# A plain first gate/up pair and down's stores issued from ScalarE's queue, in a one-core hybrid decoder step

## The chip, the cores and the metric

One core of a Trainium2 chip runs the whole program. The metric is the device time of one execution in microseconds (us). Before the change it is 1429.11 us, the median of three runs (1429.8, 1425.21, 1429.11).

## The reference

One inference step of a one-layer decoder: a mixer (gated MLP over chunks beside a Mamba-2 scan), cross-attention into 256 memory tokens, then the feed-forward network. 1024 prompt tokens and 8 sample tokens go through it (1032 columns), model width 1024, hidden width 2816, all in float32. The change is in the feed-forward network, and at its start in the norm ahead of it:

```python
def rmsnorm(x, g):
    xf = x.astype(f32)
    y = xf * lax.rsqrt(jnp.mean(xf * xf, -1, keepdims=True) + EPS)
    return (y * g.astype(f32)).astype(x.dtype)
def swiglu(hn, w_gate, w_up, w_down):
    return (jax.nn.silu(hn @ w_gate) * (hn @ w_up)) @ w_down
```

## The kernel before

**Numbers.** A float32 product is made of three fp32r matmul passes over a high and a low part of each operand (`mm3`, L170: hi by hi, hi by lo, lo by hi). Splitting an operand is a cast on ACT (the high part, L275 or L146) and a subtraction on DVE or POOL (the low part, L276 or L147).

**Where the change begins.** The last stage before the feed-forward network is cross-attention's output projection, second half (`stage(..., XO, ev_xo, name="xob")`, L1423). Its evacuation `norm_evac` (L906) adds the residual, squares, and after the eighth block asks for the norm's factor by `lagged_rstd` with the pair of lags `LAG_N = (14, 20)`, counted in matmuls that `mm3` issues: a row sum on PE (`m_csn`, L236), square root and reciprocal on ACT and DVE (`rsbn`, `rsan`, `crvn`, L219 to L224), and a spread of the factor over the partitions on PE (`m_crn`, L279). Then `quarters` (L1183) multiplies the columns by it. There are three column chunks (512, 256 and 264 wide), numbered 0, 1, 2 behind `csn3` and `crn3`. `combine(0)` makes the operands of column half q = 0 (chunk 0), `combine(1)` those of q = 1 (chunks 1 and 2).

**Gate and up** run by one level of Strassen: the hidden blocks are taken in 11 pairs, the model width in two halves, the columns in two halves q, each half of two quarters (256 wide, in q = 1 264). Seven products P1 to P7 take the place of eight. `items` (L1208) lists the work: first gate and up of pair 0 for q = 0 alone, then gate and up of pairs 1 to 10 for both q, with pair 0's q = 1 in between after pair 6. `prepare` (L1226) makes one operand of the weights two to five products ahead: sums of the four 128x512 pieces of the raw weight tiles `fr` (`ws`, L1237 to L1240, on DVE for the first four items and on POOL after), and the split into `fw`. `gate_up` (L1255) issues a product as 12 matmuls into a PSUM bank for each q (`g_..` for q = 0 and `m_..` for q = 1, X, Y, Z) and evacuates each: P1 is copied on ACT (`t`, L1283), P6, P7, P5, P4, P3 are added on DVE (L1285, L1292 to L1298), Silu is on ACT. A raw weight tile (`raw`, two buffers) comes by `load_pair` (L1220) on SP's queue.

**What down needs is made beside it.** `down_operands` (L1319) forms differences of a finished pair's hidden values (`dx`, L1324) and stores them and the values to DRAM, two DMAs for each pair and q (`x_d<-u`, `x_d<-dx`, L1331). `load_down` (L1349) loads a pair's two raw blocks of down's weights (`dr`), `down_sums` (L1356) forms sums `ds` of them and stores these (`s_d<-ds`, L1362). `dr`, `ds` and `dx` share one tag `qu` of four buffers, in rotation, so that `ds` of one pair is written where the `dx` was that the store L1331 of the pair before is still reading. All these DMAs are issued from SP's in-order queue, as are the weights' loads.

```python
                nc.sync.dma_start(x_d[i : i + m, fp, :, 256 * q : 256 * q + w].rearrange("o p n -> p o n"), src)
```

A scheduler sets each engine's order of instructions from the order in which they are written and their priorities.

Of the kernel before, what the change touches and what calls it, by code (L numbers as in the profile page):

```python
# [9 lines left out]
F32R = mybir.dt.float32r  # L10
# [7 lines left out]
P = 128  # L18
D = 1024
# [24 lines left out]
def hymba_step(ctx: ExitStack, tc: tile.TileContext, I, O):  # L44
# [55 lines left out]
    def add(w, n, k=KT):  # L100

        first = len(panels)
        panels.extend(w[j].rearrange("p (k n) -> p k n", k=k) for j in range(n))
        return first
# [9 lines left out]
    P_QA = add(I["w_q"], 8)  # L114
    P_QB = add(I["w_q"], 8)
    P_XO = [add(I["w_xo"], 8) for _ in range(2)]
    NPAIR = NF // 2

    raws, split = {}, {}
# [136 lines left out]
    def lagged_rstd(lags, use, pool, accs, ci, scale, nm):  # L256

        v = []

        def sums():  # L260
            sp = col_sums(accs, ci, nm)
            with tc.high_priority():
                v.append(pool.tile([P, len(accs), len(windows(ci))], F32, tag="crv", bufs=2, name=f"crv{nm}"))
                rstd(pool, v[0], sp, scale, nm)
            later(lags[1], rows)

        def rows():
            with tc.high_priority():
                rb = spread(v[0], ci, nm)
            use(rb)  # L270

        later(lags[0], sums)
# [630 lines left out]

    def norm_evac(accs, H, gi, XN, spill, nm, use=None, tmps=None):  # L906

        acc = {}
        pool = nrm

        def evac(j, ci, ps):
            w = CH[ci][1] - CH[ci][0]
            h = H[ci][j // 4][:, j % 4, :]
            with tc.high_priority():
                nc.vector.tensor_add(h, h, ps)
                if j == 0:
                    acc[ci] = accs[ci].tile([P, 512 if accs[ci] is nrm else w], F32, tag=f"acc{'' if accs[ci] is nrm else ci}", bufs=1, name=f"{nm}acc{ci}")
                    nc.scalar.activation(acc[ci][:, :w], h, AF.Square)
                else:
                    sq = pool.tile([P, 512], F32, tag="nsq", bufs=2, name=f"{nm}sq{ci}_{j}")  # L920
                    nc.scalar.activation(sq[:, :w], h, AF.Square)
                    eng = nc.gpsimd if j < 6 and nm == "n1" else nc.vector
                    eng.tensor_tensor(acc[ci][:, :w], acc[ci][:, :w], sq[:, :w], op=ALU.add)
            if spill is not None and j % 4 == 3:
                nc.sync.dma_start(spill[:, j - 3 : j + 1, CH[ci][0] : CH[ci][1]], H[ci][j // 4])
            if j == 7:
                lagged_rstd(LAG_N, lambda rb: (use or normed)(ci, rb[0]), pool, [[acc[ci]]], ci, 1.0 / D, f"{nm}{ci}")

        def normed(ci, rb):
            w = CH[ci][1] - CH[ci][0]  # L930
            hi = [hs(ci, F32R, f"{nm}h{ci}_{i}") for i in range(2)]
            lo = [hs(ci, F32R, f"{nm}l{ci}_{i}") for i in range(2)]
            for k in range(KT):
                i, kk = k // 4, k % 4
                tmp = n2.tile([P, 512], F32, tag=tmps[0], bufs=2, name=f"{nm}t{ci}_{k}")
                nc.vector.scalar_tensor_tensor(tmp[:, :w], H[ci][i][:, kk, :], vecT[:, k, gi : gi + 1], rb[:, :w], op0=ALU.mult, op1=ALU.mult)
                split_from(hi[i][:, kk, :], lo[i][:, kk, :], tmp[:, :w], nc.gpsimd if k % 2 else None)
            XN[ci] = xof((hi, lo))

        return evac  # L940

    quarters = None
    with ExitStack() as c2:
# [185 lines left out]

        H2 = [None] * 3  # L1130
        n3accs = [nrm] * 3
        ev_xo = norm_evac(n3accs, H2, V_FFN, None, h2_d, "n3", lambda ci, rb: quarters(ci, rb))
        XO = [lambda k, ci=ci: (OS[ci][0][k // 4][:, k % 4, :], OS[ci][1][k // 4][:, k % 4, :]) for ci in range(3)]

        def h2(ci):
# [12 lines left out]
    with ExitStack() as c3:  # L1148
# [6 lines left out]
        def piece(nm, tag="gu"):  # L1155
            return n3.tile([P, 4, 264], F32, tag=tag, bufs=4, name=nm)

        def operand(q, nm):

            if nm == ORDER[-1]:  # L1160
                return [n3.tile([P, 4, 264], F32R, tag="op", bufs=4, name=f"s{nm}{x}{q}")[:, :, : WQ[q]] for x in "hl"]
            if q == 0:
                t = hsp.tile([P, 2, 4, 256], F32R, tag="hs0", bufs=6, name=f"s{nm}0")
                return [t[:, i] for i in range(2)]
            return [hsp.tile([P, 4, 264], F32R, tag=f"hs{i}", bufs=6, name=f"s{nm}{i}1") for i in (1, 2)]
# [21 lines left out]
        def combine(q):  # L1187

            b11, b21, b12, b22 = (B[q, half, i] for half in range(2) for i in range(2))

            def part(nm, src, eng=nc.vector):
                XQ[q][nm] = operand(q, nm)
                split_from(*XQ[q][nm], src, eng)

            part("P1", b11)
            nc.vector.tensor_tensor(b11, b12, b11, op=ALU.subtract)
            part("P5", b11)
            nc.vector.tensor_tensor(b11, b22, b11, op=ALU.subtract)
            part("P6", b11)
            part("P2", b21)  # L1200
            nc.vector.tensor_tensor(b12, b22, b12, op=ALU.subtract)
            part("P7", b12)
            nc.vector.tensor_tensor(b21, b21, b11, op=ALU.subtract)
            part("P4", b21)
            part("P3", b22)


        items = [(x, 0, (0,)) for x in "gu"]  # L1208
        for fp in range(1, NPAIR):
            items += [(x, fp, (0, 1)) for x in "gu"] + ([(x, 0, (1,)) for x in "gu"] if fp == 6 else [])  # L1210
        wraw, wsum, wop = {}, {}, {}
# [9 lines left out]

        def order_of(n):

            return ORDER if n > 3 else ("P1", "P2", "P6", "P7", "P5", "P4", "P3")

        def prepare(step):  # L1226

            n, o = divmod(step, 7)
            if n >= len(items):
                return  # L1230
            load_pair(n)
            (a11, a12), (a21, a22) = ((t[:, 0:512], t[:, 512:D]) for t in wraw[n])
            nm = order_of(n)[o]
            if nm == "P6":
                eng = nc.vector if n < 4 else nc.gpsimd
                s1, s2, s3, s4 = wsum[n] = [n3.tile([P, 512], F32, tag="ws", bufs=4, name=f"ws{n}_{i}") for i in range(4)]
                eng.tensor_tensor(s1, a21, a22, op=ALU.add)  # L1237
                eng.tensor_tensor(s2, s1, a11, op=ALU.subtract)  # L1238
                eng.tensor_tensor(s4, a12, s2, op=ALU.subtract)
                eng.tensor_tensor(s3, a11, a21, op=ALU.subtract)  # L1240
            src = {"P1": a11, "P2": a12, "P4": a22}[nm] if nm in ("P1", "P2", "P4") else wsum[n][("P5", "P6", "P7", "P3").index(nm)]
            t = wp.tile([P, D], F32R, tag=("whi", "wlo")[step % 2], name=f"fw{step}")
            split_from(t[:, 0:512], t[:, 512:D], src)
            wop[step] = tuple(t[:, s].rearrange("p (k n) -> p k n", n=P) for s in (slice(0, 512), slice(512, D)))
            if o == 6:
                load_pair(n + 1)
# [69 lines left out]

        differences = []

        def down_operands(fp, q, r):  # L1319

            w = WQ[q]
            r = r.rearrange("p j h n -> p (j h) n")
            t = piece(f"dx{fp}_{q}", "qu")[:, 0:3, :w]
            sub = lambda o, x, y: nc.vector.tensor_tensor(o, x, y, op=ALU.subtract)  # L1324
            sub(t[:, 1], r[:, 3], r[:, 1])
            sub(r[:, 1], r[:, 1], r[:, 0])
            sub(t[:, 0], r[:, 3], r[:, 1])
            sub(t[:, 2], r[:, 2], t[:, 0])
            for i, src in ((0, r), (4, t)):
                m = src.shape[1]  # L1330
                nc.sync.dma_start(x_d[i : i + m, fp, :, 256 * q : 256 * q + w].rearrange("o p n -> p o n"), src)  # L1331

        def form_differences():
            for work in differences:
# [16 lines left out]
        def down_sums(fp):  # L1351

            (a11, a12), (a21, a22) = ((t[:, 0], t[:, 1]) for t in dn[fp])
            t = [n3.tile([P, 2, 512], F32, tag="qu", bufs=4, name=f"ds{fp}_{i}") for i in range(2)]
            s1, s2, s3, s4 = t[0][:, 0], t[0][:, 1], t[1][:, 0], t[1][:, 1]
            op = lambda o, x, y, k: nc.vector.tensor_tensor(o, x, y, op=k)  # L1356
            op(s1, a21, a22, ALU.add)
            op(s2, s1, a11, ALU.subtract)
            op(s3, a11, a21, ALU.subtract)
            op(s4, a12, s2, ALU.subtract)  # L1360
            for i in range(2):
                nc.sync.dma_start(s_d[2 * i : 2 * i + 2, :, fp, :].rearrange("s p n -> p s n"), t[i])  # L1362

        def prepare_down(n):

# [55 lines left out]
            return t[:, 0, i], t[:, 1, i]  # L1421

        stage(plan_of(P_XO[1], 8, first=(1, 2), last=(1, 2), chunks=(1, 2)), XO, ev_xo, name="xob")  # L1423
        for n in range(len(items)):
            gate_up(n, between_of(n))
        form_differences()
# [212 lines left out]
```

## Time and profile before

| | us |
|---|---|
| median of three runs | 1429.11 |
| the profiled execution's own time | 1433.45 |
| its span (first to last instruction) | 1431.7 |
| PE busy | 1373.5 (96%) |
| DVE busy | 967.6 (68%) |
| ACT busy | 627.3 (44%) |
| POOL busy | 365.5 (26%) |
| mean granted TensorE clock | 0.984 |

Span and time differ by what lies around the first and last instruction. In the profile's rows a start is in us from the span's start; "idle before <-releaser" is the time that an engine stood still before an instruction, and what ended it; L is a line of the program. SPq and ACTq are the queues from which DMAs are issued.

### The profile page before, as it was taken

The numbers are of one execution on the slowest core, as the hardware profiler recorded it, in microseconds if no ns is written. First come the engines' busy times: TensorE is split into PE (matmuls) and PEld (weight loads), VectorE is DVE, ScalarE is ACT, GpSimd is POOL, SyncE is SP. The second block draws the span as 40 slices with busy tenths as digits, with TensorE's granted clock in tenths as the row PEclk, the third lists the DMA queues.
The fourth block names the chain that finished last, engine by engine and source line by source line (L and its number), as shares of the span: only waits on it lengthen the run. The fifth ranks groups of instructions, "written<-read, shape, count | busy, mean of one in ns | idle before, by whom it ended". The sixth has DMA issues, their size and how long they took to land. (4 is left out here: it accounts for less than half of the span.)

```text
span 1431.7 us, 26080 instructions
## 1 busy us (share of the span) xinstructions
PE 1373.5 (96%) x10291; PEld 1308.1 (91%) x10291; DVE 967.6 (68%) x2021; ACT 627.3 (44%) x1141; POOL 365.5 (26%) x289
## 2 busy tenths in 40 slices
PE   8999999999999989999979999999899999999997
PEld 8889988899998968978979999999899999999997
DVE  7875689734524876578988766676765665655685
ACT  5666545234423545744464332232332343544654
POOL 3321122201121524320001434334443431003020
PEclk9999999999999999999999999999999999999998
DMA  8531243311733487377324554434546569655664
GB/s 301 186 96 61 91 126 104 97 45 48 248 133 99 154 288 269 106 269 276 104 89 144 170 159 138 142 118 140 170 159 201 171 189 317 206 184 171 203 194 133
DMA packets 145531, 232.67 MB, mean 163 GB/s; under 512 B 8328, under 2 KB 91880, under 8 KB 145024
## 3 DMA queue, kind: packets, MB, share of 16 engines
q1 hardware_dynamic: 145264, 230.94, 49.8%
q8 instruction: 81, 1.33, 0.4%
q14 instruction: 42, 0.34, 0.1%
q10 hardware_dynamic: 144, 0.05, 0.0%
HBM read 179.16 MB, written 51.81 MB: 161 GB/s over the span
## 5 line engine op out<-in xcount | busy, mean ns | idle before, releaser
L146 ACT CAST wh<-wr 128x1024 fp32r<-128x1024 f32 (+1 forms) x85 | 88.0, 1038 | 85.3 <-PE g_gv L170 25.1
L275 ACT CAST fw<-ws 128x512 fp32r<-128x512 f32 x96 | 59.2, 620 | 137.8 <-POOL ws L1238 61.6
L276 DVE TENSOR_TENSOR fw<-ws,fw 128x512 fp32r<-128x512 f32 x96 | 88.9, 928 | 41.3 <-ACT fw L275 41.0
L147 DVE TENSOR_TENSOR wl<-wr,wh 128x1024 fp32r<-128x1024 f32 x59 | 75.9, 1289 | 28.3 <-ACT wh L146 28.1
L147 POOL TENSOR_TENSOR wl<-wr,wh 128x1024 fp32r<-128x1024 f32 (+1 forms) x26 | 62.8, 2415 | 112.2 <-ACT wh L146 67.3
L275 ACT CAST fw<-fr 128x512 fp32r<-128x512 f32 x72 | 44.5, 618 | 79.5 <-PE m_uZ L170 20.7
L1237 POOL TENSOR_TENSOR ws<-fr 128x512 f32<-128x512 f32 x20 | 26.8, 1341 | 200.4 <-DMA fr<-in_w_gate_dram 120.8
L276 DVE TENSOR_TENSOR fw<-fr,fw 128x512 fp32r<-128x512 f32 x72 | 59.5, 826 | 9.6 <-ACT fw L275 9.1
L1542 PE MATMUL m_d<-xP,dwhi 128*128 128x264 f32 x448 | 64.1, 285 | 0.0
L276 DVE TENSOR_TENSOR dwlo<-dw,dwhi 128x1024 fp32r<-128x1024 f32 x32 | 39.8, 1245 | 35.1 <-ACT dwhi L275 35.0
L1542 PE MATMUL g_d<-xP,dwhi 128*128 128x256 f32 x448 | 63.0, 283 | 0.0
L276 DVE TENSOR_TENSOR xP<-xsP,xP 128x512 fp32r<-128x512 f32 (+2 forms) x84 | 55.0, 696 | 11.4 <-ACT xP L275 9.8
L170 PE MATMUL m_uY<-sP,fw 128*128 128x264 f32 (+1 forms) x432 | 58.4, 284 | 2.1 <-DVE fw L276 1.5
L170 PE MATMUL g_gY<-sP,fw 128*128 128x256 f32 (+1 forms) x432 | 58.4, 283 | 1.7 <-DVE t L1292 1.7
L1542 PEld LDWEIGHTS m_d<-xP,dwhi 128*128 128x128 f32 x448 | 58.5, 189 | 0.0
L1542 PEld LDWEIGHTS g_d<-xP,dwhi 128*128 128x128 f32 x448 | 57.7, 191 | 0.0
L170 PEld LDWEIGHTS m_uY<-sP,fw 128*128 128x128 f32 x432 | 54.6, 189 | 2.7 <-DVE fw L276 1.7
L170 PEld LDWEIGHTS g_gY<-sP,fw 128*128 128x128 f32 x432 | 54.3, 190 | 2.4 <-DVE t L1292 2.3
L1304 POOL TENSOR_TENSOR u<-u,g 128x512 f32<-128x512 f32 (+1 forms) x22 | 30.1, 1372 | 100.4 <-DVE u L1296 99.5
L275 ACT CAST dwhi<-dw 128x1024 fp32r<-128x1024 f32 x32 | 33.6, 1051 | 48.7 <-PE m_d L1542 38.5
L275 ACT CAST xP<-xsP 128x512 fp32r<-128x512 f32 (+2 forms) x84 | 45.2, 588 | 21.4 <-DMA xsP<-x_d 12.2
L170 PE MATMUL m_gY<-sP,fw 128*128 128x264 f32 x360 | 49.2, 285 | 4.9 <-DVE t L1292 4.9
(520 smaller groups left out, 3918.5 us busy)
## 6 DMA issues: line engine op xcount, KB each, us to landing
xsP<-x_d SPq DMA_DIRECT2D x35, 520.0 KB, 5.6
wr<-in_w_q_dram SPq DMA_DIRECT2D x24, 512.0 KB, 4.0
fr<-in_w_gate_dram SPq DMA_DIRECT2D x24, 512.0 KB, 3.6
fr<-in_w_up_dram SPq DMA_DIRECT2D x24, 512.0 KB, 3.7
dr<-in_w_down_dram SPq DMA_DIRECT2D x22, 512.0 KB, 6.4
s_d<-ds SPq DMA_DIRECT2D x22, 512.0 KB, 3.2
wr<-in_w_in_dram SPq DMA_DIRECT2D x20, 512.0 KB, 4.0
dw<-s_d SPq DMA_DIRECT2D x20, 512.0 KB, 4.5
```

The costliest lines, as they stand in the source:

```text
L146: nc.scalar.copy(hi[:, s], r[:, s])
L147: (nc.gpsimd if i == 0 or P_QA <= i < P_XO[1] else nc.vector).tensor_tensor(lo[:, s], r[:, s], f(hi[:, s]), op=ALU.subtract)
L170: ins = nc.tensor.matmul(ps, lhs(k)[a], rhs(k)[b], start=(fresh and i == 0), stop=(i == n - 1), skip_group_check=not (fresh and done))
L275: nc.scalar.copy(dst_hi, src)
L276: (eng or nc.vector).tensor_tensor(dst_lo, src, f(dst_hi), op=ALU.subtract)
L1237: eng.tensor_tensor(s1, a21, a22, op=ALU.add)
L1304: nc.gpsimd.tensor_tensor(t, t, gates[q][:, 1, :, :], op=ALU.mult)
L1542: nc.tensor.matmul(ps[:, : WQ[q]], wdn[n](k)[a], x_at(nm, q, k)[b], start=(i == 0), stop=(i == 3 * NPAIR - 1))
```

## The change

1. Pair 0, q = 0 is taken out of `items`. A new `first_pair()` runs it ahead of them without Strassen: for gate and up, each of two hidden blocks, each of two column quarters, one group of 24 matmuls (three passes over eight blocks of the model width). Its weights come as whole panels through `split_panel` (L146, L147; L148, L149 after), so no sums and no products P1 to P7 have to be made or added for it. It needs one operand more, the quarter B12, and P2, B12 and P3 ahead of the others.
2. `prepare` makes the weights' sums on DVE for two items where it was four, which are the same two items as before without the first two.
3. The second lag of the norm ahead of it goes from 20 to 44.
4. The stores of L1331 (44 DMAs) and L1362 (22 DMAs) are issued from ACT's queue.

```diff
-                lagged_rstd(LAG_N, lambda rb: (use or normed)(ci, rb[0]), pool, [[acc[ci]]], ci, 1.0 / D, f"{nm}{ci}")
+                lagged_rstd(lag, lambda rb: (use or normed)(ci, rb[0]), pool, [[acc[ci]]], ci, 1.0 / D, f"{nm}{ci}")
-        ev_xo = norm_evac(n3accs, H2, V_FFN, None, h2_d, "n3", lambda ci, rb: quarters(ci, rb))
+        ev_xo = norm_evac(n3accs, H2, V_FFN, None, h2_d, "n3", lambda ci, rb: quarters(ci, rb), lag=(14, 44))
+            if nm == "B12":
+                return [n3.tile([P, 4, 264], F32R, tag="gu", bufs=4, name=f"s{nm}{x}{q}")[:, :, : WQ[q]] for x in "hl"]
-            part("P1", b11)
+            if q == 0:
+                for nm, b in (("P1", b11), ("P2", b21), ("B12", b12), ("P3", b22)):
+                    part(nm, b)
+            else:
+                part("P1", b11)
-        items = [(x, 0, (0,)) for x in "gu"]
+        items = []
-            return ORDER if n > 3 else ("P1", "P2", "P6", "P7", "P5", "P4", "P3")
+            return ORDER if n > 1 else ("P1", "P2", "P6", "P7", "P5", "P4", "P3")
-                eng = nc.vector if n < 4 else nc.gpsimd
+                eng = nc.vector if n < 2 else nc.gpsimd
+        def first_pair():
+            for x, p0 in (("g", P_G0), ("u", P_U0)):
+                r = piece(f"{x}0_0")[:, :, :256].rearrange("p (j h) n -> p j h n", j=2)
+                for j in range(2):
+                    ahead(p0 + j)
+                    if p0 + j == P_U0:
+                        load_pair(0)
+                    if p0 + j == P_U0 + 1:
+                        for s in range(3):
+                            prepare(s)
+                    hi, lo = split[p0 + j]
+                    for half in range(2):
+                        ps = (gbank, mbank)[half](f"{x}0_{j}_{half}")
+                        ops = [XQ[0][nm] for nm in (("P1", "P2"), ("B12", "P3"))[half]]
+                        mm3(ps[:, :256], lambda k: (hi[:, k, :], lo[:, k, :]), lambda k: tuple(t[:, k % 4, :] for t in ops[k // 4]), range(KT))
+                        with tc.high_priority():
+                            if x == "g":
+                                nc.scalar.activation(r[:, j, half, :], ps[:, :256], AF.Silu)
+                            else:
+                                nc.vector.tensor_mul(r[:, j, half, :], gates[0][:, j, half, :], ps[:, :256])
+                gates[0] = r if x == "g" else None
+            differences.append(lambda: down_operands(0, 0, r))
-                nc.sync.dma_start(x_d[i : i + m, fp, :, 256 * q : 256 * q + w].rearrange("o p n -> p o n"), src)
+                nc.scalar.dma_start(x_d[i : i + m, fp, :, 256 * q : 256 * q + w].rearrange("o p n -> p o n"), src)
-                nc.sync.dma_start(s_d[2 * i : 2 * i + 2, :, fp, :].rearrange("s p n -> p s n"), t[i])
+                nc.scalar.dma_start(s_d[2 * i : 2 * i + 2, :, fp, :].rearrange("s p n -> p s n"), t[i])
+        first_pair()
```

The scheduler decides what this does to the orders. Three places follow.

PE at the start of the feed-forward network, before. `g_gZ0_0` and `m_uX0_0` are products of pair 0's gate and up, `m_csn32` and `m_crn32` the row sum and the spread of chunk 2's norm factor, `m_crn31` the spread of chunk 1's.

```order
L170 MATMUL g_gY0_0_7880<-sP40_7307,fw5_7827 128x256 x12
L170 MATMUL g_gZ0_0_7967<-sP3h0_7310,fw6_7844 128x256 x4
L170 MATMUL g_gZ0_0_7967<-sP3l0_7311,fw6_7844 128x256 x4
L170 MATMUL g_gZ0_0_7967<-sP3h0_7310,fw6_7844 128x256 x4
L279 MATMUL m_crn31_0_7762<-ident_72,crvn31_7728 128x128 x2
L236 MATMUL m_csn32_7853<-ones_77,n3acc2_7358 128x1 x3
L279 MATMUL m_crn32_0_7891<-ident_72,crvn32_7857 128x128 x3
L170 MATMUL m_uX0_0_8022<-sP10_7288,fw7_7877 128x256 x12
```

The same place now; `g_u0_1_0` is the plain group of up's hidden block 1, column quarter 0. From the row of `m_csn32` to that of `m_crn32` there are 18 rows of 4 matmuls; the first and the last rows of that stretch are:

```order
L238 MATMUL m_csn32_7830<-ones_77,n3acc2_7362 128x1 x3
L172 MATMUL m_g0_0_1_7854<-sB12h0_7323,wh84_7657 128x256 x4
L172 MATMUL m_g0_0_1_7854<-sP3h0_7327,wh84_7657 128x256 x4
```

```order
L172 MATMUL g_u0_1_0_8062<-sP10_7317,wl87_7986 128x256 x4
L172 MATMUL g_u0_1_0_8062<-sP20_7320,wl87_7986 128x256 x4
L281 MATMUL m_crn32_0_7897<-ident_72,crvn32_7834 128x128 x3
L172 MATMUL m_g0_1_1_7958<-sB12h0_7323,wh85_7794 128x256 x4
```

Chunk 2's row sum and the spread of its factor stood next to each other on PE; now 72 matmuls of 256 columns stand between them.

SP through one pair, before: stores of pair 4 (`u4`, `dx4`; the last digit is q), the loads and sums of down's pair 5, and gate/up's weights `fr11`, `fr12`.

```order
L1220 DMA fr11_0_10151<-in_w_up_dram 128x1024
L1331 DMA x_d_102<-u4_0_9870 128x4x256
L1349 DMA dr5_0_10367<-in_w_down_dram 128x1024
L1220 DMA fr11_1_10152<-in_w_up_dram 128x1024
L1349 DMA dr5_1_10368<-in_w_down_dram 128x1024
L1331 DMA x_d_102<-dx4_0_10252 128x3x256
L1331 DMA x_d_102<-u4_1_9871 128x4x264
L1331 DMA x_d_102<-dx4_1_10259 128x3x264
L1362 DMA s_d_103<-ds5_0_10503 128x2x512
L1220 DMA fr12_0_10402<-in_w_gate_dram 128x1024
L1362 DMA s_d_103<-ds5_1_10504 128x2x512
```

The same pair now, on SP and then on ACT (`fr9` and `fr10` are the same weights, the items being two fewer):

```order
L1231 DMA fr9_0_10123<-in_w_up_dram 128x1024
L1384 DMA dr5_0_10339<-in_w_down_dram 128x1024
L1231 DMA fr9_1_10124<-in_w_up_dram 128x1024
L1384 DMA dr5_1_10340<-in_w_down_dram 128x1024
L1231 DMA fr10_0_10374<-in_w_gate_dram 128x1024
```

```order
L1366 DMA x_d_102<-u4_0_9842 128x4x256
L1294 COPY t00_10081<-g_gX5_0_10092 128x256
L1294 COPY t01_10084<-m_gX5_1_10106 128x264
L277 CAST fw62_10120<-ws8_3_9946 128x512
L1366 DMA x_d_102<-dx4_0_10224 128x3x256
L1366 DMA x_d_102<-u4_1_9843 128x4x264
L1366 DMA x_d_102<-dx4_1_10231 128x3x264
L277 CAST fw63_10155<-fr9_0_10123 128x512
L1299 ACTIVATE g5_0_10087<-g_gX5_0_10092 128x256
```

On SP the load `dr5_0` now follows the load of `fr9_0` directly; on ACT the store of `u4_0` stands ahead of both copies of P1, and three stores ahead of the next cast. SP's list has 423 rows where it had 489, ACT's 1158 where it had 1104.

## Rows read from the trace of the kernel before

**Rows 1.** The profile's page, busy time and share of the span by engine.

```profile
PE 1373.5 (96%) x10291; PEld 1308.1 (91%) x10291; DVE 967.6 (68%) x2021; ACT 627.3 (44%) x1141; POOL 365.5 (26%) x289
```

**Rows 2.** Windows by stage: PE, PEld, DVE, ACT, POOL busy (instructions), PEclk, DMA share, GB/s.

```profile
718.00:787.00 69.00, 58.56 (x474) 57.89 (x474) 60.49 (x115) 35.65 (x58) 6.57 (x6) 0.95 0.35 116
787.00:1140.00 353.00, 339.75 (x2782) 335.31 (x2781) 232.73 (x415) 106.66 (x209) 138.09 (x103) 1.00 0.50 159
1140.00:1196.00 56.00, 56.00 (x469) 56.00 (x468) 37.20 (x66) 20.26 (x37) 18.47 (x14) 1.00 0.66 199
```

**Rows 3.** Timeline of PE, 730 to 744 us, around the norm's last spread.

```profile
730.32 0.73 PE L236 MATMUL m_csn<-ones,n3acc 128*128 128x1 f32 x6
739.09 0.87 PE L279 MATMUL m_crn<-ident,crvn 128*128 128x128 f32 x3 [8.04 <-DVE crvn L224]
739.61 2.67 PE L170 MATMUL m_uX<-sP,fw 128*128 128x256 f32 x12
742.12 1.60 PE L170 MATMUL m_uY<-sP,fw 128*128 128x256 f32 x12
743.56 1.24 PE L170 MATMUL m_uZ<-sP,fw 128*128 128x256 f32 x9
```

**Rows 4.** Timelines of ACT and of DVE, 730 to 740 us.

```profile
736.12 1.05 ACT L275 CAST sP<-B 128x1056 fp32r<-128x1056 f32 x1
```

```profile
731.80 3.22 DVE L1183 SCALAR_TENSOR_TENSOR B<-H,vecT,m_crn 128x256 f32<-128x256 f32 x8
737.20 1.26 DVE L276 TENSOR_TENSOR sP<-B,sP 128x1056 fp32r<-128x1056 f32 x1 [1.42 <-ACT sP L275]
...
739.09 0.69 DVE L1237 TENSOR_TENSOR ws<-fr 128x512 f32<-128x512 f32 x1
```

**Rows 5.** PE's waits, 760 to 1200 us: total, times, longest.

```profile
PE m_gY L170 <- DVE t L1292: 4.9, 6, 1.7
...
PE g_uY L170 <- DVE t L1292: 1.5, 2, 1.0
...
PE g_gZ L170 <- DVE g L1294: 1.1, 6, 0.2
```

**Rows 6.** DVE's waits, 760 to 1200 us.

```profile
DVE ds L1356 <- DMA x_d<-dx: 34.8, 8, 6.5
```

**Rows 7.** Timeline of SP, 872 to 905 us: one pair's DMA issues.

```profile
877.04 0.38 SPq L1331 DMA_DIRECT2D x_d<-u  x1
...
880.46 0.42 SPq L1331 DMA_DIRECT2D x_d<-dx  x1
...
881.46 1.93 SPq L1331 DMA_DIRECT2D x_d<-dx  x1
```

**Rows 8.** Timelines of DVE, PE and ACT in the same pair.

```profile
888.76 0.78 DVE L1356 TENSOR_TENSOR ds<-dr 128x512 f32<-128x512 f32 x1 [6.48 <-DMA x_d<-dx]
892.89 0.42 DVE L1292 TENSOR_TENSOR t<-t,m_gY 128x264 f32<-128x264 f32 x1
```

```profile
880.74 1.59 PE L170 MATMUL g_gX<-sP,fw 128*128 128x256 f32 x12
893.36 1.73 PE L170 MATMUL m_gY<-sP,fw 128*128 128x264 f32 x12 [1.73 <-DVE t L1292]
```

```profile
876.59 0.37 ACT L1283 COPY t<-g_gX 128x256 f32<-128x256 f32 x1 [0.81 <-PE g_gX L170]
```

**Rows 9.** Windows of two us in the same pair (columns as in rows 2).

```profile
879.00:881.00 2.00, 2.00 (x19) 2.00 (x19) 1.93 (x6) 0.06 (x1) 0.00 (x0) 1.00 1.01 270
...
887.00:889.00 2.00, 2.00 (x19) 2.00 (x18) 0.24 (x1) 0.00 (x0) 1.92 (x2) 1.00 1.03 329
```

**Rows 10.** The line L1331, and the one DMA that ACT issues.

```profile
DMA to landing us min/median/max: 2.6/8.1/10.3
```

```profile
0.80 0.40 ACTq L84 DMA_DIRECT2D vecT<-in_vecs_dram  x1
1.23 1.28 ACT L302 ACT_TABLE_LOAD   x1 [1.23 <-PEq L1628]
```

More of the change, by code (lines that the diff above doesn't have):

```diff
@@ L116, in hymba_step @@
     P_XO = [add(I["w_xo"], 8) for _ in range(2)]
+    P_G0 = add(I["w_gate"], 2)
+    P_U0 = add(I["w_up"], 2)
     NPAIR = NF // 2
@@ L901, in hymba_step, with norm_evac @@
         stage([([(P_GU + j, j)], (0, 1, 2)) for j in range(2)] + [([(P_GU + j, j) for j in (2, 3)], (0, 1, 2))], X, ev_um, name="gu")
-    def norm_evac(accs, H, gi, XN, spill, nm, use=None, tmps=None):
+    def norm_evac(accs, H, gi, XN, spill, nm, use=None, tmps=None, lag=LAG_N):
         acc = {}
@@ L1199, in combine @@
             part("P6", b11)
-            part("P2", b21)
+            if q == 1:
+                part("P2", b21)
             nc.vector.tensor_tensor(b12, b22, b12, op=ALU.subtract)
@@ L1204, in combine @@
             part("P4", b21)
-            part("P3", b22)
-        items = [(x, 0, (0,)) for x in "gu"]
+            if q == 1:
+                part("P3", b22)
+        items = []
         for fp in range(1, NPAIR):
```

## The prediction

> **What bounds the kernel now.** First the page's busy times: PE works 96% of the span and every other engine at most 68% [rows 1], so an edit is worth what it takes off PE's work or off PE's idle time. Then the windows by stage show where the idle time lies. In the start of the feed-forward network (718 to 787 us) PE is busy 58.56 of 69.00, so 10.44 us are lost; in gate and up (787 to 1140) 339.75 of 353.00, so 13.25; from 1140 to 1196 it is busy throughout [rows 2]. Those two losses are all that this change can win back. Next the timeline of the first: one gap of 8.04 us, in which PE waits for the last norm factor [rows 3]. The clock granted in this stage is 0.95 of full speed where later it is 1.00 [rows 2]: after the gap the twelve matmuls of `m_uX` hold PE until the next twelve start, 742.12 - 739.61 = 2.51 us, while those next twelve take 743.56 - 742.12 = 1.44 [rows 3], another 1.07 lost. Last PE's waits in the second stretch, and what stands behind them: the longest are waits for the DVE addition `t` of P7 [rows 5], and DVE was late because it stood 34.8 us in eight pairs before `ds`, waiting for the store `x_d<-dx` to let go of a buffer [rows 6].
>
> **One pair, to see that chain.** The store of `u` is issued at 877.04 and six more DMAs follow by 881.46 on the same queue (first, fifth and last are shown [rows 7]). They are 512 KB (`u`, both `dr`, `fr`), 384 (`dx`), 528 and 396 KB: 3356 KB. The DMA engines are busy all this while, at 1.01 to 1.03 in the windows shown [rows 9]. DVE starts `ds` at 888.76 after 6.48 us of waiting, behind it come the additions, the last at 892.89, and PE starts `m_gY` 1.73 us late at 893.36 [rows 8].
>
> **The change, part by part.**
>
> Arithmetic. The first pair for q = 0 takes 2 x 2 x 2 groups of 24 = 192 matmuls where Strassen took 2 x 7 x 12 = 168. A matmul of 256 columns is 1.44 / 12 = 0.120 us [rows 3], so 24 more cost 24 x 0.120 = **+2.9**, all on PE, which nothing hides.
>
> The gap before the norm's spread. Before, nothing of PE's stands between the row sum and the spread; now 72 matmuls do, 72 x 0.120 = 8.6 us, more than the 8.04 of the gap [rows 3]. That the chain itself grows is unlikely: before, it shared ACT with table loads (1.28 each [rows 10]) and a cast (1.05), and DVE with eight multiplications (3.22) and a split (1.26) [rows 4]. DVE loses here 8 sums and 14 splits at 0.69 and 11 evacuations at 0.42, 19.8 us, and gains four panel splits and one of B12 at about 1.26, and four evacuations at 0.42: 8.0 [rows 4, 8]. I take **-8.0** for the gap and, since PE then doesn't stand still before, **-1.1** for the clock.
>
> What is late next. The 10.44 - 8.04 = 2.4 us of other idle time in this stage will not stay as it is. The items that follow now start their sums and casts behind the plain panels, on a raw buffer that comes free only when the last panel is split. Laying the new order on the durations, I find PE early in three places: twice where an operand of q = 1 waits for its cast and split (1.05 + 1.26 [rows 4]), 1.8 and 1.9 us, and once where a cast stands behind the first store in ACT's queue, 0.8. That is an estimate of 4.5 us, so **+2.1** against 2.4; its bounds are none left (-2.4) and as much again as the gap (+8). The three sums of the first stage: 2.9 - 8.0 - 1.1 + 2.1 = **-4.1**, from -8.6 (all 11.5 us gone, 2.9 paid) to +2.9 plus little.
>
> The later lag (20 to 44) only places the spread; it is the 72 matmuls above, and I cost it at nothing beyond them. The operands made earlier are the same work; B12 is one cast and one split more, in the 8.0 above.
>
> The stores leave SP's queue. Three things follow. `dr_0` no longer stands behind the store of `u`, which waits for DVE; what it waits for itself are the transfers of the pair before, so it goes right behind the load that precedes it, and its 512 KB are out of the crowd: 2844 KB are left. The loads of weights don't stand behind the stores of `ds` any more. And `dx_0` has on its own queue only `u_0` ahead of it. The 3356 KB from 877.04 to 888.76 moved at 286 KB/us [rows 7, 8]; if `dx` lands with the last byte of 2844 KB it is there at 877.04 + 9.9 = 887.0, and if it lands with `u_0`, itself and the two loads beside them (512 + 384 + 512 + 512 = 1920 KB) at 883.8. When does it have to land? From the start of `ds` to the end of the last addition are 892.89 + 0.42 - 888.76 = 4.55 us, and PE would have been ready at 893.36 - 1.73 = 891.63 [rows 8], so `ds` must start by 887.1. Even the late end meets that, just; the early one by 3 us. The waits that hang on this are 4.9 + 1.5 + 1.1 = 7.5 [rows 5]; I take 7 of them, and 1 of the 13.25 - 7.5 = 5.7 that remain, where casts wait for weights that came late. That is **-8.0**, from 0 to -13.25.
>
> What the issue costs on ACT. On SP an issue takes about 0.4 us, and 1.93 at the longest in this pair [rows 7]; the only DMA that ACT issues before the change takes 0.40, and ACT's next instruction starts 0.03 later [rows 10]. So 66 issues hold ACT for 66 x 0.4 = 26 us, spread over 400 us in which it is busy 107 of 353 [rows 2]. In the pair shown the store of `u` would go at 877.04, and the copy of P1, at 876.59 before [rows 8], behind it at 877.4: 0.8 us later. Its bank is wanted by PE at 880.74, and the copy ends at 877.8, 2.9 us ahead. The casts behind the other three stores are two products ahead of PE. I cost the issues at 0; the bounds are no loss and the 1.6 us a pair of the third rival. An in-order queue also takes in what the stores wait for, but these are DVE's differences of the same moment, and on SP the last three stores are issued within 1.0 us, from 880.46 to 881.46 [rows 7].
>
> From 1140 us on PE is busy without a gap [rows 2], and the order of its work there is the same: 0.
>
> **Sum.** -4.1 - 8.0 = -12.1. The profiled execution took 1433.45, which gives 1421.35; it lies 4.3 above the median of the runs, 1429.11, from which the same sum gives **1417.0**.
>
> **The rivals.** *The stores land no sooner.* The DMA engines are near 1.0 in the windows shown [rows 9], and a store's landing took 8.1 at the median [rows 10]; a second queue only mixes the same packets, `dx_0` shares with both loads and lands when it did. For it: the share. Against: `dr_0` is out of the crowd, which the bytes above show to be enough. Then only the first stage wins: 1429.1 - 4.1 = 1425.0. The Trainium skill, page "DMA: Bandwidth & Descriptors", section "Issuing engines are not separate DMA queues", says that DMAs started by ScalarE or SyncE run on the same 16 engines and interleave, and that starting them from several engines only saves the sequencer's time. By that rule the second term would be 0 as far as it rests on bandwidth; the trace agrees with its premise in the shares near 1.0, but what I count on is mostly the order in SP's queue.
>
> *The first stage wins nothing.* The norm's chain is late again behind panel splits, or the waits of q = 1 eat the gap: 2.9 paid, 0 won, and the stores' 8.0: 1429.1 + 2.9 - 8.0 = 1424.0. For it: DVE is busy 60.5 of 69 us there [rows 2]; against it, the 11.8 us of work that DVE loses on balance.
>
> *ACT is held by the stores* (slower). If an issue on ACT takes what the longest took on SP, 1.93 instead of 0.42 [rows 7], three of them in a row hold ACT 3 x 1.5 = 4.5 us longer; of that 2.9 are covered (the margin of the copy), so 1.6 reach PE in each pair, in 11 pairs 17.6. The stores then land no sooner either. 17.6 - 4.1 = +13.5: 1442.6. It decides from the point where ACT loses more than 2.9 us in a pair. For it: the long issues come when the engines are full, which they still are; against it, only four stores are under way in ACT's queue where SP's had seven DMAs.
>
> *The change doesn't do what it says*: both first rivals at once, 1429.1 + 2.9 = 1432.0.
>
> **How the numbers follow.** Forecast 0.70; stores no sooner 0.11; first stage wins nothing 0.08; ACT held 0.08; both 0.03. A measurement of this kernel can tell 0.3%, 4.3 us. Faster by more than that are the forecast and the second rival (-5.1): 0.78. Within it are the first rival (-4.1) and the last (+2.9): 0.14. Slower: 0.08. The range begins at 1409, where the first stage gives its 8.6 and the second 11.5, and reaches to 1427, past the first two rivals; left out are ACT held, the last rival, and the far ends of the bounds.
>
> **What would show it.** Right: 718 to 787 loses the gap before `m_crn`, and the granted clock there stays near 1.00; DVE's wait for `x_d<-dx` falls from 34.8 to under 10, and PE's idle time in gate and up from 13.25 to about 5; SP issues the first `dr` several us before the store of `u`. Wrong: `ds` still waits as long; PE waits for ACT's copy `t` or casts `fw` by more than a few us, with issues of over 1 us on ACT's queue; or a new gap of several us stands at the first product of pair 1.

## The result, and the profile after

The changed kernel takes 1414.76 us (median; 1412.13 to 1418.92), the one before 1429.45: the ratio is 0.9894 with a 95% interval from 0.9875 to 0.9914. That is 14.7 us less, where 12.1 were forecast.

The page's busy times after, and the DMA queue of ACT, q10:

```profile
PE 1372.5 (97%) x10315; PEld 1309.3 (93%) x10315; DVE 961.9 (68%) x1997; ACT 622.4 (44%) x1129; POOL 362.7 (26%) x287
...
q10 hardware_dynamic: 26544, 32.09, 6.7%
```

PE has its 24 more matmuls, and yet no more busy time than in [rows 1]; 32 MB have moved to ACT's queue. The windows by stage (columns as in [rows 2]), the first stage in two pieces:

```profile
716.00:745.00 29.00, 29.00 (x246) 29.00 (x246) 21.60 (x46) 15.86 (x24) 0.00 (x0) 1.00 0.31 93
745.00:785.00 40.00, 38.03 (x311) 37.40 (x311) 33.39 (x57) 14.48 (x25) 8.05 (x6) 1.00 0.38 127
785.00:1125.00 340.00, 334.39 (x2757) 333.03 (x2756) 234.71 (x410) 106.66 (x207) 137.63 (x103) 0.99 0.51 164
```

In the first stage 1.97 us of PE's time are idle where it was 10.44, and the granted clock is 1.00 where it was 0.95; in gate and up 5.61 where it was 13.25 [rows 2]. PE's timeline around the norm's last spread shows where the gap of [rows 3] went:

```profile
722.96 0.73 PE L238 MATMUL m_csn<-ones,n3acc 128*128 128x1 f32 x6
723.54 0.73 PE L172 MATMUL m_g<-sB12h,wh 128*128 128x256 f32 x4
...
731.25 1.12 PE L172 MATMUL g_u<-sP,wl 128*128 128x256 f32 x8
732.21 0.49 PE L281 MATMUL m_crn<-ident,crvn 128*128 128x128 f32 x3
```

The plain groups run from 723.54 to 732.21, and `m_crn` starts with no wait. Waits, 760 to 1200 us (engine, waiting line, releaser: total, times, longest), PE's and then DVE's for the stores:

```profile
PE g_gX L172 <- ACT fw L277: 2.2, 1, 2.2
PE g_uX L172 <- ACT t L1294: 1.1, 1, 1.1
...
PE g_uY L172 <- DVE t L1303: 0.6, 1, 0.6
```

```profile
DVE ds L1391 <- DMA x_d<-dx: 18.3, 6, 3.5
```

The six waits of `m_gY` for P7's addition `t`, at the head of [rows 5], have left PE's list; of `g_uY`'s two one of 0.6 is left. DVE's wait for `x_d<-dx` is half of [rows 6], no less. In one pair, the first `dr` on SP's queue, and then ACT:

```profile
859.45 0.37 SPq L1384 DMA_DIRECT2D dr<-in_w_down_dram  x1
```

```profile
868.06 0.37 ACTq L1366 DMA_DIRECT2D x_d<-u  x1
868.47 0.37 ACT L1294 COPY t<-g_gX 128x256 f32<-128x256 f32 x1 [1.66 <-DVE u L1359]
```

The first `dr` goes 8.6 us ahead of the store of `u`, where in [rows 7] it went behind it; the copy of P1 stands behind that store.

**A measure for what follows.** The stretch from the first matmul of gate and up to the last group of matmuls of pair 10's P3 (from the start of its first row to the start of its last) holds nearly all that the change touches. Its first and last row of PE in the kernel before, after, and in two of the runs below:

```profile
718.06 1.59 PE L170 MATMUL g_gX<-sP,fw 128*128 128x256 f32 x12
...
1195.75 0.65 PE L170 MATMUL m_uZ<-sP3h,fw 128*128 128x264 f32 x4
```

```profile
716.55 2.08 PE L172 MATMUL g_g<-sP,wh 128*128 128x256 f32 x16
...
1177.26 0.64 PE L172 MATMUL m_uZ<-sP3h,fw 128*128 128x264 f32 x4
```

The plain pair alone:

```profile
716.78 2.07 PE L172 MATMUL g_g<-sP,wh 128*128 128x256 f32 x16
...
1187.68 0.64 PE L172 MATMUL m_uZ<-sP3h,fw 128*128 128x264 f32 x4
```

The stores alone:

```profile
713.83 1.59 PE L170 MATMUL g_gX<-sP,fw 128*128 128x256 f32 x12
...
1181.25 0.64 PE L170 MATMUL m_uZ<-sP3h,fw 128*128 128x264 f32 x4
```

The stretch takes 477.69 us before, 460.71 after, 470.90 and 467.42 in the two halves. Below it is called the stretch, each from one profiled execution. It shows gains that are 0.8 to 2.3 us larger than those of the medians (17.0 against 14.7 for the whole change), and how far it varies from one execution to the next was not measured.

### The profile page after: what moved, and what is told of

It is laid out like the page before. It is cut to its first block, busy times and chain, and to the rows that moved or that the text cites. A ratio compares the mean times of both kernels' runs of the same rounds, so it can differ in the third digit from the quotient of the medians.

```text
span 1413.3 us, 26087 instructions
## 1 busy us (share of the span) xinstructions
PE 1372.5 (97%) x10315; PEld 1309.3 (93%) x10315; DVE 961.9 (68%) x1997; ACT 622.4 (44%) x1129; POOL 362.7 (26%) x287
## 4 chain that ended last, share of the span: by engine, by line
PE 74%; DVE 12%; DMA 8%; issue 2%; ACT 2%; POOL 2%; SPq 0%; DVEq 0%; POOLq 0%; ACTq 0%
PE m_d L1578 8%; PE g_d L1578 8%; PE g_wo L172 6%; PE g_xbc L172 6%; PE g_xob L172 3%; PE g_gu L172 3%; PE g_z L172 3%; PE m_uY L172 3%; PE g_uY L172 3%; PE m_gY L172 2%; PE g_gY L172 2%; PE g_xoa L172 2%; PE m_uX L172 2%; DVE fw L278 2%; PE g_uX L172 2%
## 5 line engine op out<-in xcount | busy, mean ns | idle before, releaser
L148 ACT CAST wh<-wr 128x1024 fp32r<-128x1024 f32 (+1 forms) x89 | 92.2, 1038 | 84.2 <-PE g_gv L172 25.1
L278 DVE TENSOR_TENSOR fw<-ws,fw 128x512 fp32r<-128x512 f32 x88 | 85.4, 972 | 32.6 <-ACT fw L277 32.5
L277 ACT CAST fw<-ws 128x512 fp32r<-128x512 f32 x88 | 54.6, 622 | 114.2 <-POOL ws L1249 47.1
L149 DVE TENSOR_TENSOR wl<-wr,wh 128x1024 fp32r<-128x1024 f32 x63 | 79.7, 1268 | 28.2 <-ACT wh L148 26.5
L149 POOL TENSOR_TENSOR wl<-wr,wh 128x1024 fp32r<-128x1024 f32 (+1 forms) x26 | 62.4, 2402 | 111.7 <-ACT wh L148 72.6
L277 ACT CAST fw<-fr 128x512 fp32r<-128x512 f32 x66 | 40.8, 618 | 88.2 <-PE m_uZ L172 20.2
L277 ACT CAST xP<-xsP 128x512 fp32r<-128x512 f32 (+2 forms) x84 | 45.2, 588 | 25.6 <-DMA xsP<-x_d 16.1
L172 PE MATMUL m_uY<-sP,fw 128*128 128x264 f32 x396 | 54.3, 286 | 0.3 <-DVE fw L278 0.3
L172 PE MATMUL g_gY<-sP,fw 128*128 128x256 f32 (+1 forms) x396 | 53.0, 283 | 1.1 <-DVE t L1296 1.1
L172 PEld LDWEIGHTS m_uY<-sP,fw 128*128 128x128 f32 x396 | 50.9, 191 | 0.6 <-DVE fw L278 0.6
L172 PEld LDWEIGHTS g_gY<-sP,fw 128*128 128x128 f32 x396 | 49.7, 190 | 1.4 <-DVE t L1296 1.3
L172 PE MATMUL g_uY<-sP,fw 128*128 128x256 f32 x360 | 48.2, 283 | 0.6 <-DVE t L1303 0.6
```

Of the source, the lines that this page charges most:

```text
L148: nc.scalar.copy(hi[:, s], r[:, s])
L149: (nc.gpsimd if i == 0 or P_QA <= i < P_XO[1] else nc.vector).tensor_tensor(lo[:, s], r[:, s], f(hi[:, s]), op=ALU.subtract)
L172: ins = nc.tensor.matmul(ps, lhs(k)[a], rhs(k)[b], start=(fresh and i == 0), stop=(i == n - 1), skip_group_check=not (fresh and done))
L277: nc.scalar.copy(dst_hi, src)
L278: (eng or nc.vector).tensor_tensor(dst_lo, src, f(dst_hi), op=ALU.subtract)
```

## The experiments

**The two halves.** The first undoes the stores in the change, the second does the stores alone in the kernel before:

```diff
-                nc.scalar.dma_start(x_d[i : i + m, fp, :, 256 * q : 256 * q + w].rearrange("o p n -> p o n"), src)
+                nc.sync.dma_start(x_d[i : i + m, fp, :, 256 * q : 256 * q + w].rearrange("o p n -> p o n"), src)
-                nc.scalar.dma_start(s_d[2 * i : 2 * i + 2, :, fp, :].rearrange("s p n -> p s n"), t[i])
+                nc.sync.dma_start(s_d[2 * i : 2 * i + 2, :, fp, :].rearrange("s p n -> p s n"), t[i])
```

> The change with all stores back on SP's queue: only the plain first pair and the lag are left. Theory (two gains that add up: about 5 us at the norm's gap, the rest in gate and up): about 1424, 0.3 to 0.4% faster than before, no gap before the last m_crn, and DVE's wait for x_d<-dx near the 34.8 us of before. Rival (the stores win nothing, all of the 14.7 us come from the first pair): about 1415, as the whole change.

> The kernel before with the 66 stores issued from ACT's queue and nothing else. Theory: about 1420, 0.6 to 0.7% faster, with the 8 us gap before m_crn still there and DVE's wait for x_d<-dx halved as in the whole change (18.3). Rival (the stores win nothing): 1429.

Measured: 1424.81 for the pair alone, ratio 0.9960 [0.9949, 0.9972], and 1421.01 for the stores alone, 0.9936 [0.9917, 0.9955], against 1430.49. The gains are 5.7 and 9.5 us, together 15.2 where the whole has 14.7; in the stretch 6.79 + 10.27 = 17.06 where the whole has 16.98. They add up and neither is the other's cover. With the stores alone the 8.0 us before `m_crn` are still there, and DVE's wait for the stores is halved (17.0 us); with the pair alone DVE still waits for the stores:

```profile
PE m_crn L279 <- DVE crvn L224: 8.0, 1, 8.0
```

```profile
DVE ds L1391 <- DMA x_d<-dx: 37.2, 8, 6.2
```

**The lag.** Edit of the change: `lag=(14, 44)` back to `lag=(14, 20)`.

> The whole change with the norm's second lag back at 20. Theory: the 72 plain matmuls that the scheduler puts between m_csn32 and m_crn32 cover the chain at either lag, as the lag only places the spread: within 2 us of 1414.5, and no gap before m_crn. Rival (the lag is what closes the gap): a gap of several us before m_crn is back and the time is 1418 to 1422.

Measured: 1415.38, ratio 0.9888 [0.9867, 0.9908], the stretch 461.86, and no wait at `m_crn`. The number is not what closes the gap; the plain groups are.

**Which stores.** First by tensor: `x_d` alone on ACT, then `s_d` alone (one of the two lines above each).

> The change with the s_d stores back on SP: only x_d's 44 stores are on ACT. Theory (it is x_d's place ahead of dr and fr on SP's queue that cost): within 2 us of the whole change, 1413 to 1417. Rival (the loads of fr behind the stores of ds cost as much): half of the stores' gain lost, about 1419 to 1420.

> The change with the x_d stores back on SP: only s_d's 22 stores are on ACT. Theory: as with all stores on SP, 1423 to 1425, with DVE's wait for x_d<-dx near 35 us. Rival (fr behind ds): about 1419 to 1420.

Measured: 1414.51, ratio 0.9892 [0.9872, 0.9912], for `x_d`: the whole gain. And 1426.96, 0.9975 [0.9960, 0.9990], for `s_d`: nothing beyond the plain pair, if anything 2 us worse (the stretch 474.55 against 470.90). So the 22 stores of `s_d` need not have moved.

Then within `x_d`: the stores of `dx` alone on ACT (`s_d` too), those of `u` alone (`s_d` too), and at last `u`'s 22 stores and nothing else (the second edit below, with `s_d` back on SP).

```diff
-                nc.scalar.dma_start(x_d[i : i + m, fp, :, 256 * q : 256 * q + w].rearrange("o p n -> p o n"), src)
+                (nc.scalar if i else nc.sync).dma_start(x_d[i : i + m, fp, :, 256 * q : 256 * q + w].rearrange("o p n -> p o n"), src)
```

```diff
-                nc.scalar.dma_start(x_d[i : i + m, fp, :, 256 * q : 256 * q + w].rearrange("o p n -> p o n"), src)
+                (nc.sync if i else nc.scalar).dma_start(x_d[i : i + m, fp, :, 256 * q : 256 * q + w].rearrange("o p n -> p o n"), src)
```

> The whole change with the stores of u back on SP, where each stands ahead of the load dr_0 again; only the stores of dx (and of ds) are on ACT. Theory (dr's early start is most of the gain): dr_0 is issued behind the store of u as before, DVE waits for x_d<-dx 25 us or more, gate and up win at most half of their 10 us: 1419 to 1424. Rival (dx must only get out from behind the loads): the wait falls to 20 us or less, 1414 to 1417.

> The other half: the stores of u on ACT, those of dx on SP behind the loads dr and fr. Theory (dr's early start): dr_0 is issued right behind the load ahead of it, and most of the gain stays: 1414 to 1419, with DVE's wait for x_d<-dx at 15 to 25 us. Rival (dx's own queue): the wait is 30 us or more and the time 1421 to 1425.

> The plain first pair with only the 22 stores of u on ACT's queue; the stores of dx and of ds stay on SP. Theory (the store of u, which waits for DVE, must not stand ahead of dr_0 on SP's queue; the other 44 moves change nothing): 1413 to 1417, the whole gain. Rival (u alone carries only a part, and ds's stores ahead of fr cost once dx's are on SP too): 1418 to 1422.

Measured: `dx` on ACT 1430.53, ratio 1.0005 [0.9993, 1.0017], worse than forecast by either theory: even the plain pair's gain is gone. `u` on ACT 1415.62, 0.9907 [0.9892, 0.9922]. `u` only, 1416.90, 0.9905 [0.9891, 0.9920], with a stretch of 459.76 where the change has 460.71. A third of the DMAs that the change moves carries its gain. The run with `dx` on ACT has `s_d` there too, and `s_d` alone had already lost 2 us: the stretches of the two are alike, 474.12 and 474.55. Why its median is another 3.6 us longer stays open; DVE waits 38.9 us for the stores, where the pair alone has 37.2.

**Why, in one pair.** In their source the plain pair alone and `u` only differ in nothing but the queue of 22 stores. SP, POOL, DVE and PE in the same pair of the plain pair alone:

```profile
869.92 0.38 SPq L1366 DMA_DIRECT2D x_d<-u  x1
870.40 0.45 SPq L1384 DMA_DIRECT2D dr<-in_w_down_dram  x1
871.02 0.83 SPq L1231 DMA_DIRECT2D fr<-in_w_up_dram  x1
```

```profile
877.50 1.29 POOL L1248 TENSOR_TENSOR ws<-fr 128x512 f32<-128x512 f32 x1 [7.06 <-DMA fr<-in_w_up_dram]
...
881.83 1.74 POOL L1251 TENSOR_TENSOR ws<-fr,fr 128x512 f32<-128x512 f32 x1
```

```profile
880.01 0.70 DVE L1391 TENSOR_TENSOR ds<-dr 128x512 f32<-128x512 f32 x1 [4.85 <-DMA x_d<-dx]
...
882.34 1.78 DVE L278 TENSOR_TENSOR fw<-ws,fw 128x512 fp32r<-128x512 f32 x1
884.04 0.42 DVE L1303 TENSOR_TENSOR t<-t,m_gY 128x264 f32<-128x264 f32 x1
```

```profile
867.82 1.59 PE L172 MATMUL g_gX<-sP,fw 128*128 128x256 f32 x12
...
884.51 1.72 PE L172 MATMUL m_gY<-sP,fw 128*128 128x264 f32 x12 [0.68 <-DVE t L1303]
```

And with `u`'s stores on ACT:

```profile
861.65 0.37 SPq L1384 DMA_DIRECT2D dr<-in_w_down_dram  x1
871.36 0.33 SPq L1231 DMA_DIRECT2D fr<-in_w_up_dram  x1
```

```profile
876.16 1.29 POOL L1248 TENSOR_TENSOR ws<-fr 128x512 f32<-128x512 f32 x1 [5.37 <-ACT g L1299]
...
880.14 1.75 POOL L1251 TENSOR_TENSOR ws<-fr,fr 128x512 f32<-128x512 f32 x1
```

```profile
879.25 1.48 DVE L1391 TENSOR_TENSOR ds<-dr 128x512 f32<-128x512 f32 x1 [3.71 <-DMA x_d<-dx]
...
882.36 0.68 DVE L278 TENSOR_TENSOR fw<-ws,fw 128x512 fp32r<-128x512 f32 x1
882.96 0.42 DVE L1303 TENSOR_TENSOR t<-t,m_gY 128x264 f32<-128x264 f32 x1
```

```profile
868.17 1.59 PE L172 MATMUL g_gX<-sP,fw 128*128 128x256 f32 x12
...
884.02 1.60 PE L172 MATMUL m_gY<-sP,fw 128*128 128x264 f32 x12
```

Count from P1's first matmul (`g_gX`). The load `fr` is issued 3.2 us after it in both, but with the 512 KB of `dr` already through it lands sooner: POOL's first sum `ws`, which waited for it at 9.68, now starts at 7.99 and no longer for a DMA. `ds` starts at 11.08 instead of 12.19. So the last addition `t` starts at 14.79 instead of 16.22, 1.43 sooner, and PE's 0.68 us are gone. Of these 1.43 us 1.11 are the earlier `ds`. The other 0.32 lie between `ds` and `t`, which are 3.71 apart instead of 4.03. There the split `fw` takes 0.68 us instead of 1.78: in the first kernel POOL's last sum runs from 881.83 to 883.57, across it; in the second POOL has ended at 881.89, before it begins. But `ds` itself, now beside POOL's third sum (878.88 to 880.18), takes 1.48 instead of 0.70. The Trainium skill, page "SBUF — State Buffer", section "SBUF: two separate sides", says that VectorE and GpSimd share one pair of ports under an exclusive lock, held for a whole instruction, which a VectorE operation with two inputs in SBUF needs while a GpSimd operation reads SBUF; the two durations of the same split, 0.68 and 1.78, agree with it. The slow split is not what PE's stall hangs on, though. In the changed kernel, where `ds` starts sooner still, the split of the same pair is slow again, and PE has no wait for `t`:

```profile
878.84 1.77 DVE L278 TENSOR_TENSOR fw<-ws,fw 128x512 fp32r<-128x512 f32 x1
```

One more thing differs between the two kernels than the queue: the scheduler gave DVE another order. In the pair alone both of the last sums `ds` stand ahead of the next additions `g` (L1305); with `u` only one `g` stands between them. The pair alone, then `u` only:

```profile
885.59 0.68 DVE L1391 TENSOR_TENSOR ds<-dr,ds 128x512 f32<-128x512 f32 x1
886.19 0.41 DVE L1305 TENSOR_TENSOR g<-t,g_gZ 128x256 f32<-128x256 f32 x1
```

```profile
884.51 0.41 DVE L1305 TENSOR_TENSOR g<-t,g_gZ 128x256 f32<-128x256 f32 x1
884.84 0.68 DVE L1391 TENSOR_TENSOR ds<-dr,ds 128x512 f32<-128x512 f32 x1
```

The kernels with `u`'s stores on SP's queue have the first order in such pairs, the kernel before among them, and those with `u`'s stores whole on ACT's queue the second. Up to `t` both orders are the same, so the stall at `m_gY` is not the order's. Counted from P1, PE starts `m_gY` at 15.85 with `u` only instead of 16.69, 0.84 sooner, and the product that waits for `g` 1.30 sooner (17.29 instead of 18.83, less two matmuls that the scheduler put ahead of it). So up to about a third of what the pair wins may be the order's; no run holds the order fixed.

**Two queues, or an early load.** All stores back on SP, and in their place the loads `dr` on ACT, where they stand behind the copy of P1:

```diff
-                nc.sync.dma_start(dn[fp][i].rearrange("p j n -> p (j n)"), I["w_down"][2 * fp + i])
+                nc.scalar.dma_start(dn[fp][i].rearrange("p j n -> p (j n)"), I["w_down"][2 * fp + i])
```

> All stores back on SP's queue, and in their place the 22 loads dr of down's weights on ACT's queue, where they stand behind the copy of P1, so they start no sooner than before. Theory (what helps is that dr starts early and is out of the crowd, not that there are two queues): DVE's wait for x_d<-dx stays above 25 us and the time at 1421 to 1426, near the plain pair alone (1424.8). Rival (two queues side by side let dx land sooner by themselves): the wait falls to about 18 us as in the whole change and the time to 1413 to 1417.

Measured: 1427.20, ratio 0.9977 [0.9965, 0.9990], about a us above what the theory said; DVE waits 28.7 us for the stores. Two queues side by side, with the loads `dr` behind the copy of P1, win nothing over the plain pair alone (1424.81). But this is not because `ds` came late. In the six pairs like the one above it starts 11.1 to 12.1 us after P1, much as with `u` only (10.7 to 12.7) and sooner than with the pair alone (12.0 to 13.6), and in four of them PE has no wait for `t`. What is late are the weights: POOL's first sum starts 10.0 to 10.2 us after P1, where it starts at 7.7 to 8.9 with `u` only and at 9.2 to 10.5 with the pair alone. And PE waits for the additions `g`, which here stand behind both `ds`:

```profile
PE g_gZ L172 <- DVE g L1305: 5.4, 7, 1.4
```

So an early `ds` is not enough by itself. The weights that land late and DVE's order stand beside it, and this run does not tell these two apart.

**ACT's margin.** Each store of `x_d` cut into its pieces, 14 issues a pair on ACT instead of 4:

```diff
-                nc.scalar.dma_start(x_d[i : i + m, fp, :, 256 * q : 256 * q + w].rearrange("o p n -> p o n"), src)
+                for o in range(m):
+                    nc.scalar.dma_start(x_d[i + o, fp, :, 256 * q : 256 * q + w], src[:, o])
```

> The whole change with each store of x_d cut into one DMA for each of its pieces, so 14 issues a pair on ACT instead of 4, some 4 us more of ACT's queue in one stretch. Theory (ACT's margin to PE was put at 2.9 us, and only the first store's 4 issues, 1.1 us more, stand before the copy of P1): within 3 us of 1414.5. Rival (ACT is close to holding PE): 10 more issues at 0.37 us reach PE at least in part, 1.5 us or more in each of 11 pairs, 1430 or more.

Measured: 1418.64, ratio 0.9920 [0.9895, 0.9945]: 3.9 us more than the change, a little over the theory's 3 and far from the rival's 15. The two intervals overlap, but the stretch says the same, 464.85 against 460.71. An issue takes 0.34 (`u`) and 0.39 us (`dx`) at the median. The loss is not spread over the pairs: from P1 to P1, three of the five pairs ahead of the two short items grow by only 0.1 us, while 3.7 us are lost from 989 to 1059 us, around the short items, and 2.2 won back behind them. DVE's order changed too (all four `ds` now stand ahead of the addition `t` for `m_gY`), so 3.9 us is not the price of the issues alone. DVE's wait for the stores fell further, to 5.1 us, and the time still rose; so that wait is not what bounds the changed kernel.

**What is left.** The largest loss in the changed kernel is at 1000 to 1020 us, in the two short items (pair 0, q = 1), which ask for their weights, casts and sums in half the time. Two tries, pair 0's sums for down made elsewhere, and the short items run after pair 2:

```diff
-        sums_at |= {items.index(("u", 0, (1,))): 0,
+        sums_at |= {items.index(("g", 4, (0, 1))): 0,
```

```diff
-            items += [(x, fp, (0, 1)) for x in "gu"] + ([(x, 0, (1,)) for x in "gu"] if fp == 6 else [])
+            items += [(x, fp, (0, 1)) for x in "gu"] + ([(x, 0, (1,)) for x in "gu"] if fp == 2 else [])
```

> The whole change with pair 0's sums for down made in item g of pair 5 in place of the short item u of pair 0, where DVE is late and PE waits 2.2 us and then runs at a granted clock of 0.91. Theory (DVE's four ds in the short item hold the cast that PE waits for): that wait and the clock's fall go, 1409 to 1413. Rival (the loads of the short items' weights set the wait): no change or slower by what the sums cost in the other item, 1414 to 1418.

(The edit puts the sums into item g of pair 4, not 5.)

> The whole change with pair 0's second half (its two short items) run after pair 2 in place of pair 6, to see whether the loss around 1000 us, some 39 matmuls' time in 20 us, belongs to the short items or to that moment. Theory (the short items ask for their weights, casts and sums in half the time): the loss moves with them to some 830 us and the time is unchanged within 2 us, 1413 to 1417. Rival (that moment's stores and loads set it): 1409 to 1412.

Measured: 1416.62, ratio 0.9901 [0.9885, 0.9917], for the sums: no gain, the time that the rival gave. But the wait that the theory named, PE's 2.2 us for a cast, is gone; in its place PE waits 3.1 us for `t` in the next pair, behind a `ds` that waits 4.2 us for its load `dr` where it waited 1.5 in the change. So the rival's reason is not shown either. 1414.51, 0.9894 [0.9877, 0.9911], for the items: the same time, and the loss went with them. The windows of the change, and then of this run:

```profile
1000.00:1020.00 20.00, 17.51 (x130) 17.08 (x129) 15.90 (x22) 7.77 (x15) 10.34 (x7) 0.91 0.44 142
```

```profile
840.00:860.00 20.00, 17.59 (x131) 17.17 (x130) 15.46 (x23) 6.99 (x14) 9.70 (x7) 0.91 0.43 136
...
1000.00:1020.00 20.00, 20.00 (x169) 20.00 (x168) 13.98 (x26) 5.01 (x9) 10.15 (x8) 1.00 0.28 88
```

A full window holds 169 matmuls; 130 and 131 are left where the short items run. The loss belongs to them. No run was faster than the change by more than its interval.

## Why the prediction was right

**The arithmetic and the gap.** Forecast -4.1 for the first stage, measured -5.7 by the medians of the pair alone (-6.79 in its stretch). The term of the gap was right: the 72 matmuls cover the chain, no wait is left at `m_crn`, and the granted clock is back at 1.00. The term that was mis-sized is "what is late next": 4.5 us were put to three places found by laying the new order on the durations; 1.97 are left in the change, and 1.47 in the pair alone (716 to 785 us). 4.5 - 1.47 = 3.0 is a little more than the 2.7 us by which the stretch beat the forecast. Of the three places PE's waits show little: 0.3 us for an operand of q = 1, and in the change 0.5 for a cast. The longest wait left, 1.1, is for an addition on DVE that was not among them.

**The stores.** Forecast -8.0, measured -9.5 (-10.27 in the stretch). The three ways were named: `dr` early and out of the crowd, weights no longer behind the stores, `dx` behind `u` alone. The runs show that the store of `u` has to leave SP's queue, which lets `dr` go early, and that this is enough; the other two are worth nothing without it: with `s_d` moved alone, with `dx` and `s_d` moved, or with `dr` on a second queue but late there is no gain. How much of it comes by the earlier `ds`, by weights that land sooner and by DVE's other order is not separated: no run issues `dr` early with `u`'s stores left on SP's queue. The prediction had `ds` start at 883.8 to 887.0 instead of 888.76, 1.8 to 5 us sooner, and DVE's wait fall under 10 us. P1 of the pair in the kernel before, P1 and `ds` in the changed one:

```profile
874.96 1.59 PE L170 MATMUL g_gX<-sP,fw 128*128 128x256 f32 x12
```

```profile
865.99 1.59 PE L172 MATMUL g_gX<-sP,fw 128*128 128x256 f32 x12
```

```profile
876.39 0.82 DVE L1391 TENSOR_TENSOR ds<-dr 128x512 f32<-128x512 f32 x1 [3.03 <-DMA x_d<-dx]
```

Counted from P1, `ds` starts at 13.80 before [rows 8], at 12.19 with the pair alone, at 11.08 with `u` only and at 10.40 in the change: 3.4 us sooner than before, in the middle of what was forecast. The step that failed is the one from there to the waits and the stall, though its size was nearly right. DVE's wait fell to 18.3, not under 10. DVE is ready at 888.76 - 6.48 = 882.28 [rows 8], so even the early end, 883.8, leaves 1.5 us of wait in a pair, about 12 in eight. And the late end would not have been enough: the deadline, 887.1, is 12.1 after P1, and in four pairs of the pair alone `ds` starts at 12.0 to 12.2 and PE waits 0.5 to 0.7 us for `t`. Behind `ds` the prediction had only DVE's additions; POOL's sums of the weights it had as 1 us of late casts, and DVE's order it took as given. What it left out worked the same way, so the nearness of -8.0 to -9.5 is in part luck.

**The issues on ACT.** Costed at 0, with the copy of P1 0.8 us later and 2.9 us of margin. The copy starts 2.48 us after P1's first matmul (868.47 - 865.99) where it was 1.63 (876.59 - 874.96 [rows 8]): 0.85 later, and PE doesn't wait in this pair; its one wait for such a copy is 1.1 us where it was 0.7 before. That the change with 66 issues takes no longer than `u` only with 22 (1414.76 and 1416.90) shows the issues to be near free. With 14 instead of 4 stores of `x_d` in a pair the kernel takes 3.9 us more, of which the issues are only one possible cause.

**The rivals.** "The stores land no sooner" gave 1425.0, which is what the pair alone takes, and it fell: the same 16 engines carry the same bytes, and still 22 issues on another queue gave 8 us (1424.81 to 1416.90). The rule of the Trainium skill that was cited for it (page "DMA: Bandwidth & Descriptors", section "Issuing engines are not separate DMA queues") speaks of bandwidth and of the sequencer's time; what was won here is neither, but the order behind a DMA that waits for an engine. "The first stage wins nothing" fell by the pair alone, "ACT is held" by the change, where an issue of `x_d`'s stores took 0.37 us at the median and 1.06 at the longest, not 1.93, and by the 14 issues: 1418.64 where it put 1442.6.

## What to carry to other kernels

On an in-order queue look for the DMA that waits for an engine, and at what stands behind it: moving that one kind elsewhere gave all that moving every store gave. A wait's total is not its price: 31.3 us of waits (`u` only) came with 6.1 us of idle PE in gate and up, and 28.7 (`dr` on ACT) with 15.3, because what counts is the moment at which what stands behind them ends, against the engine that bounds. And where a scheduler sets the orders, moving a DMA to another queue can change the order of an engine that has nothing to do with it: compare the orders before the times are read as an effect of the queue. Where a serial chain leaves the bounding engine idle, work that needs none of the chain's results can be worth more than the fewer operations of a better algorithm: 24 more matmuls (2.9 us) bought 8 us of gap and 1 of clock.

## What was not expected of the hardware

A window's idle time understates a stall. Before the change, 880 to 900 us shows 17.72 us of busy PE, 2.28 idle, but 143 matmuls where a full window has 169; 26 at 0.119 us are 3.1:

```profile
880.00:900.00 20.00, 17.72 (x143) 17.09 (x142) 11.99 (x22) 5.86 (x12) 5.95 (x4) 1.00 0.69 224
```

Over the stretch idle time fell by 16.1 us and the clock gave back 1.1, yet 17.0 were gained with 2.9 paid for the added matmuls, 19.9 in all; the rest is likely of this kind.

The same split of 128x512 takes DVE 0.68 us alone and 1.78 while POOL works on a sum of its own (both shown above). An earlier load does not take the overlap away, it moves it: with `u` only it is `ds` that takes 1.48 instead of 0.70, and in the change the split takes 1.77 again.

What runs ahead of gate and up is nearly the same program in all these kernels, and yet gate and up begins anywhere from 713.83 to 718.82 us in their profiled executions. A single profiled time therefore says less about an edit than the stretch does: the stores alone took 1418.79 in theirs, against a median of 1421.01.
